# Strassen products for the second half's q, k and v; gates and the first projection as the attentions' filling

## The chip, the cores and the metric

The kernel runs on one core of one Trainium2 chip. A core has five engines, each with its own stream of instructions: TensorE (PE, matrix products and transpositions into PSUM), VectorE (DVE), ScalarE (ACT), GpSimd (POOL) and SyncE (SP, which here only issues transfers). They wait for each other through semaphores. The metric is the time on the device in microseconds, as the median of several runs; one further execution was profiled.

## The reference

One layer of an encoder on 2048 tokens with 1024 features, in float32. Cut to what matters:

```python
h = rms_norm(x, norm_mix)
z = h @ w_in                      # (2048, 1024) @ (1024, 4352)
q_a, k_a, v_a, q_b, k_b, v_b, g_a, g_b = split(z)   # 512,128,128,512,512,512,1024,1024
y_a = windowed_gqa(q_a, k_a, v_a, sink)       # 8 heads, 2 kv heads, |t-s| <= 128, ALiBi, sink logit
y_b = neighborhood_attn(q_b, k_b, v_b, rpb)   # 8 heads, 8 x 16 neighbours on a 32 x 64 grid, bias
gates = sigmoid(concat(g_a, g_b) + b_gate)
merged = gates[:, :1024] * (y_a @ w_proj_a) + gates[:, 1024:] * (y_b @ w_proj_b)
x = x + merged @ w_out
x = x + square(relu(rms_norm(x, norm_mlp) @ w_up)) @ w_down
return rms_norm(x, norm_final)
```

## The kernel before

**Arithmetic.** A float32 operand is held as a pair of `fp32r` numbers, high and low, and a product is three matmuls into one bank: high·high, high·low, low·high (`mm3`, lines 200 to 202, and `mm3s`, lines 284 to 286). So one "product" of a 128x128 weight tile and 512 tokens is always one matmul on each of three lines. Splitting a number in its pair costs a copy on ACT and a subtraction on DVE or POOL.

**Blocks.** The tokens lie in four blocks of 512 (`b` = 0 to 3). The first half is blocks 0 and 1, the second half 2 and 3.

**Dense stage (to 359.5 us).** For blocks 0 and 1, all columns of `w_in` come from "quads": a quad takes 512 columns (one takes 256) and both blocks, and forms the four quarter results with seven half-size products instead of eight (Strassen). `QUADS` lists them: k of A, q of A, q of B, k of B, v of B, four quads of gates. `in_seeded` runs a quad's products 1, 5, 6, 2, 7, 3, 4. Its right-hand operands are "pages" (`in_page[n]`, tiles `zh<n>`), one pair for each product `n`, made once from the normalised and transposed x; `in_left` makes the weight side (`zwhl`), `in_result` writes the results to DRAM. Beside the quads, `wo_parts` prepares `w_out` (in quads 2, 3, 7, 8), and in quads 5 and 6 blocks 2 and 3 of x are normalised and transposed into DRAM (`h1d`).

**Windowed attention A (359.5 to about 672 us) and neighbourhood attention B (to 1059.6 us)**, 32 units each (`attn_a`, `attn_b`). A unit computes scores on PE (bank `s`), bias and maximum on DVE, exponentials on ACT, normalisation on POOL, then for every 128 keys transposes on PE (bank `pt`), splits the result on ACT and DVE (`ph`, `pl`; in B `phb`, `plb`), and multiplies by v (bank `av`). `drive` starts units two ahead of the one that is finished. **Filling**: q, k, v and the gates of blocks 2 and 3 are computed during the attentions. `qk_tile`, `v_tile` and `gate_tile` are generators for 128 columns each; a generator loads its weights, splits them, then makes a piece of 24 matmuls (`feature_tile`, bank `mm`, with copy and store) for each of the two blocks, by full products. Their pages `hT` are loaded from `h1d`, scaled and split by `h_pages` at the start of A. `chain` strings the generators together and loads two ahead; `paced` puts one piece after the other into the program, each after the end of a stated unit (`done[at]`). The kernel's scheduler then sets the order of the instructions on each engine. In A there are 24 pieces, in B 44.

**Merge (1059.6 to 1393 us).** In two passes (`m` = 0: blocks 0 and 1, `m` = 1: blocks 2 and 3). `gated(f, n)` multiplies 128 columns of `w_proj_a` (n = 0) or `w_proj_b` (n = 1) by `y_a` or `y_b` (`load_y`), reads the gates from `zg`, applies the sigmoid, multiplies; the two are added to the pages `m0` to `m3`. Then `merged @ w_out` follows by Strassen (banks `b`, operands `pgl`), with the residual (`beside_out`). In pass 1, DVE also transposes the rows of the first pass for the MLP (`turned_out`, tiles `ht`, line 247) between the gated products.

**MLP.** The up stage runs to 2014 us, the down stage to the end; both are untouched.

## Time and profile before

| | us |
|---|---|
| median of 3 runs | 2634.39 (2632.62 to 2640.43) |
| profiled execution, its own time | 2636.0 |
| its span | 2634.2 |
| dense stage, after its start-up | 45 to 359.5 |
| attention A with the passage to it | 359.5 to about 672 |
| attention B | about 672 to 1059.6 |
| merge | 1059.6 to 1393 |
| up, down | 1393 to 2014, 2014 to 2634 |

In rows by windows, each engine's column is its busy time in the window and, in brackets, its instructions; then come the granted TensorE clock (1.00 is full), the mean busy share of the 16 DMA engines and the GB/s moved. With a tile's name given, only instructions on that tile are counted. In rows by groups stand line, engine, operation, output<-inputs, shapes and count, then busy us and mean ns of one, then the idle time just before them and what ended it. In rows of waits: engine, line, what was waited for, us in total, times, longest.

### The profile page before, as it was taken

The numbers are of one execution on the slowest core, as the hardware profiler recorded it, in microseconds if no ns is written. First come the engines' busy times: TensorE is split into PE (matmuls) and PEld (weight loads), VectorE is DVE, ScalarE is ACT, GpSimd is POOL, SyncE is SP. The second block draws the span as 40 slices with busy tenths as digits, with TensorE's granted clock in tenths as the row PEclk, the third lists the DMA queues.
The fourth block names the chain that finished last, engine by engine and source line by source line (L and its number), as shares of the span: only waits on it lengthen the run. The fifth ranks groups of instructions, "written<-read, shape, count | busy, mean of one in ns | idle before, by whom it ended". The sixth has DMA issues, their size and how long they took to land. (4 is left out here: it accounts for less than half of the span.)

```text
span 2634.2 us, 34479 instructions
## 1 busy us (share of the span) xinstructions
PE 2577.0 (98%) x12044; PEld 2138.2 (81%) x12044; DVE 1626.5 (62%) x2611; ACT 1290.9 (49%) x2319; POOL 374.1 (14%) x477
## 2 busy tenths in 40 slices
PE   8999999999999999999999999999999999999998
PEld 6878877787888888878887888888887888888887
DVE  7965566665444444465687677776656634554766
ACT  7445456666555555344246555644444322322444
POOL 0001233334555552000000000000000000000011
PEclk9999999999999999999999999999999999999999
DMA  5777785446777664777687655854427825444554
GB/s 184 246 245 205 237 277 148 116 125 177 212 222 198 174 186 138 268 240 235 202 296 239 237 204 199 283 200 148 149 103 289 314 98 183 147 147 169 184 192 168
DMA packets 349950, 525.94 MB, mean 200 GB/s; under 512 B 29624, under 2 KB 173112, under 8 KB 347600
## 3 DMA queue, kind: packets, MB, share of 16 engines
q1 hardware_dynamic: 333008, 483.88, 57.4%
q10 hardware_dynamic: 13248, 28.32, 2.9%
q0 software_dynamic: 3520, 11.54, 1.2%
q8 instruction: 95, 1.56, 0.2%
q14 instruction: 79, 0.65, 0.1%
HBM read 349.51 MB, written 174.13 MB: 199 GB/s over the span
## 5 line engine op out<-in xcount | busy, mean ns | idle before, releaser
L285 PE MATMUL b<-dwh,dah 128*128 128x512 f32 x896 | 349.0, 389 | 0.4 <-DVE dwh L281 0.4
L286 PE MATMUL b<-dwh,dah 128*128 128x512 f32 x896 | 348.1, 389 | 0.0
L284 PE MATMUL b<-dwh,dah 128*128 128x512 f32 x896 | 338.2, 389 | 1.7 <-ACT dwh L280 1.7
L280 ACT CAST dah<-da 128x1024 fp32r<-128x1024 f32 (+1 forms) x128 | 120.8, 945 | 368.3 <-PE b L286 250.3
L281 DVE TENSOR_TENSOR dah<-da,dah 128x1024 fp32r<-128x1024 f32 (+1 forms) x128 | 139.8, 1094 | 223.3 <-ACT dah L280 221.7
L284 PE MATMUL b<-ubh,uwhlb 128*128 128x512 f32 x592 | 232.1, 392 | 6.0 <-ACT uwhlb L280 4.4
L285 PE MATMUL b<-ubh,uwhlb 128*128 128x512 f32 x592 | 231.6, 391 | 0.6 <-DVE ubh L281 0.6
L286 PE MATMUL b<-ubh,uwhlb 128*128 128x512 f32 x592 | 229.7, 390 | 0.0
L200 PE MATMUL mm<-hT,whl 128*128 128x512 f32 x544 | 219.1, 403 | 3.5 <-ACT hT L754 3.5
L201 PE MATMUL mm<-hT,whl 128*128 128x512 f32 x544 | 215.2, 396 | 0.6 <-DVE hT L755 0.6
L202 PE MATMUL mm<-hT,whl 128*128 128x512 f32 x544 | 215.5, 396 | 0.0
L284 PEld LDWEIGHTS b<-dwh,dah 128*128 128x128 f32 x896 | 168.1, 188 | 36.9 <-ACT dwh L280 2.1
L285 PEld LDWEIGHTS b<-dwh,dah 128*128 128x128 f32 x896 | 168.2, 188 | 35.7 <-DVE dwh L281 0.8
L286 PEld LDWEIGHTS b<-dwh,dah 128*128 128x128 f32 x896 | 168.2, 188 | 34.8
L284 PE MATMUL zb<-zh,zwhl 128*128 128x512 f32 x476 | 187.1, 393 | 4.5 <-DVE zc L277 1.8
L285 PE MATMUL zb<-zh,zwhl 128*128 128x512 f32 x476 | 186.9, 393 | 0.0
L286 PE MATMUL zb<-zh,zwhl 128*128 128x512 f32 x476 | 185.6, 392 | 0.8 <-DVE zwhl L281 0.8
L277 DVE TENSOR_TENSOR uc<-b,uc 128x512 f32<-128x512 f32 x160 | 109.5, 690 | 122.7 <-PE b L286 116.5
L284 PEld LDWEIGHTS b<-ubh,uwhlb 128*128 128x128 f32 x592 | 111.8, 189 | 30.3 <-ACT uwhlb L280 4.8
L285 PEld LDWEIGHTS b<-ubh,uwhlb 128*128 128x128 f32 x592 | 111.9, 189 | 24.1 <-DVE ubh L281 1.0
L286 PEld LDWEIGHTS b<-ubh,uwhlb 128*128 128x128 f32 x592 | 111.4, 188 | 23.4
L200 PEld LDWEIGHTS mm<-hT,whl 128*128 128x128 f32 x544 | 102.9, 189 | 21.9 <-ACT hT L754 4.4
(268 smaller groups left out, 5838.6 us busy)
## 6 DMA issues: line engine op xcount, KB each, us to landing
at<-uc SPq DMA_DIRECT2D x224, 256.0 KB
da<-at SPq DMA_DIRECT2D x96, 512.0 KB
dw<-in_w_down_dram SPq DMA_DIRECT2D x160, 256.0 KB
uraw<-in_w_up_dram SPq DMA_DIRECT2D x32, 1024.0 KB
pgl<-wo_d SPq DMA_DIRECT2D x28, 1024.0 KB
raw<-in_w_in_dram SPq DMA_DIRECT2D x34, 512.0 KB
zraw<-in_w_in_dram SPq DMA_DIRECT2D x16, 1024.0 KB
z<-zg SPq DMA_DIRECT2D x64, 256.0 KB
```

Source lines behind the costliest of these rows:

```text
L200: PE.matmul(ps, lh, rh, start=first, stop=False)
L201: PE.matmul(ps, lh, rl, start=False, stop=False)
L202: PE.matmul(ps, ll, rh, start=False, stop=last)
L277: return eng.tensor_tensor(out=out, in0=a, in1=b, op=op).ins
L280: A.copy(hi, src)
L281: return eng.tensor_tensor(out=lo, in0=src, in1=hi.bitcast(F32), op=ALU.subtract).ins
L284: PE.matmul(ps, lh, rh, start=first, stop=False, skip_group_check=True)
L285: PE.matmul(ps, lh, rl, start=False, stop=False, skip_group_check=True)
L286: PE.matmul(ps, ll, rh, start=False, stop=last, skip_group_check=True)
```

## The change

The gates' and the first half's quads stay as they are, in another order. Five more quads follow for blocks 2 and 3: q of A, q of B, k of B, v of B, k and v of A. For their pages, x of blocks 2 and 3 is normalised and transposed two quads earlier (in quads 3 and 4); `h1_sums` reads `h1d` back in quads 5 to 7, forms the four sums and differences that Strassen needs and stores them (`h1s`); `h1_right` refills the pages in quad 8, the last one on the first half, product by product behind their last use; `h1_last` loads one more page that the gates of block 3 need. `w_out` is prepared in the later quads, the tables of B's bias in quad 11.

The filling is now 16 gate tiles for blocks 2 and 3, on the quads' pages, and then 8 `proj_tile`s: 128 columns of `w_proj_a` by `y_a`, all four blocks, two blocks (24 matmuls) a piece, multiplied by the gate and stored in DRAM as `zp`. 22 pieces lie in A, 26 in B. The merge multiplies by `w_proj_b` alone and adds `zp`.

A gate is no longer stored raw: ACT stores tanh of half its argument (`half_tanh`), and a sigmoid is half of that plus one. The "plus one" is an operand of the DVE multiplication, the half is a scale of 0.5 in the attentions' normalisation on POOL. Lastly, A loads K and V of both groups of heads at its start and takes its units in the order of groups 1, 0 throughout.

The diff, cut to its core:

```diff
+    def half_tanh(out, z, f):
+        A.activation(out, z, AF.Tanh, scale=0.5, bias=bg[:, f : f + 1])
...
-    QUADS = [(O_KA, P), (O_QA, 256), (O_QB, 256), (O_KB, 256), (O_VB, 256)]
-    QUADS += [(O_GA + n * BT, 256) for n in range(4)]
+    gate_quads = [(O_GA + n * BT, 256) for n in range(4)]
+    QUADS = [(O_KA, P), (O_QA, 256), (O_QB, 256), *gate_quads[:2], (O_KB, 256), (O_VB, 256), *gate_quads[2:]]
+    SECOND = len(QUADS)
+    QUADS += [(O_QA, 256), (O_QB, 256), (O_KB, 256), (O_VB, 256), (O_KA, P)]
...
+    G.tensor_scalar(bg[:, 0:16], bg[:, 0:16], 0.5, 1.0, ALU.mult, ALU.mult)
...
+    def h1_sums(k):
+        lo, hi = own(), own()
+        for t, p in ((lo, 0), (hi, 1)):
+            for j in range(2):
+                SY.dma_start(t[:, j * BT : (j + 1) * BT], h1d[j][p * BT + k * P : p * BT + (k + 1) * P, :])
...
+        for n, out, x, y in ((5, b11, b12, b11), (7, b12, b22, b12), (6, b22, b22, b11), (4, b21, b21, b22)):
+            yield
+            add(V, out, x, y, ALU.subtract)
+            G.dma_start(h1s[n][k * P : (k + 1) * P, :], out)
+    def h1_right(out):
+        for n in ORDER_3:
+            yield
+            b, p = {1: (0, 0), 2: (0, 1), 3: (1, 1)}.get(n, (None, None))
+            out[n] = h1_page(n, h1s[n]) if b is None else h1_page(n, h1d[b][p * BT : (p + 1) * BT], p)
...
-    h_pages(2)
-    def qk_tile(col, scale, tiled=False):
...
-    def v_tile(col):
...
-            G.tensor_scalar(s[:, h, lo:hi], s[:, h, lo:hi], ri[:, h : h + 1], 1.0, ALU.mult, ALU.mult)
+            G.tensor_scalar(s[:, h, lo:hi], s[:, h, lo:hi], ri[:, h : h + 1], 0.5, ALU.mult, ALU.mult)
...
+    def proj_tile(f):
+        raw = load_slice([(cols(w_pa[0], f * P), 4)])
+        yield
+        hl = T(wp, [P, 2, KC, P], F32R, "whl", 2)
+        split(raw[:, 0:4], hl[:, 0, 0:4], hl[:, 1, 0:4], V)
+        yield
+        for b in (0, 2):
+            z = T(wp, [P, 2, BT], F32, "z", 3)
+            for j in range(2):
+                SY.dma_start(z[:, j], zg[b + j][0][f * P : (f + 1) * P, :])
+            for j in range(2):
+                if ypages[b + j] is None:
+                    y_page(b + j)
+                hi, lo = ypages[b + j]
+                ps = psum("mm", 2)
+                for c in range(4):
+                    mm3(ps, hl[:, 0, c, :], hl[:, 1, c, :], hi[:, c], lo[:, c], c == 0, c == 3)
+                V.scalar_tensor_tensor(out=z[:, j], in0=z[:, j], scalar=1.0, in1=ps, op0=ALU.add, op1=ALU.mult)
+                put(zp[b + j][f], z[:, j])
+            yield
...
-    dense = [qk_tile(O_KA, 1.0), v_tile(O_VA)]
...
-    dense += [gate_tile(f, (2, 3)) for f in range(16)]
+    fill = [gate_tile(f, (2, 3)) for f in range(16)] + [proj_tile(f) for f in range(8)]
...
-    drive((attn_a(g, i) for g in (1, 0) for i in range(7)), live, False)
-    paced(fill, range(12), 24, 3)
...
-    drive((attn_a(g, i) for g in range(2) for i in range(7, 16)), live, True)
-    paced(fill, range(12, 24), 24, 3)
+    load_kv(1, 0)
+    load_kv(1, 1)
+    load_kv(0, 0)
+    load_kv(0, 1)
+    drive((attn_a(1, i) for i in range(14)), live, False)
+    paced(fill, range(11), 22, 3)
+    drive((attn_a(g, i) for g in (1, 0) for i in range(14 if g else 0, 16)), live, True)
+    paced(fill, range(11, 22), 22, 3)
...
-    paced(fill, range(20), 38, 4)
+    paced(fill, range(11), 21, 3)
...
-    paced(fill, range(20, 44), 38, 4)
+    paced(fill, range(11, 26), 21, 3)
...
-                V.tensor_tensor(out=g[:, j], in0=ps, in1=g[:, j], op=ALU.mult)
-            gates[f, n] = g
+                V.scalar_tensor_tensor(out=g[:, j], in0=g[:, j], scalar=1.0, in1=ps, op0=ALU.add, op1=ALU.mult)
+            add(V, ms[f // 2][:, f % 2], ga, g)
```

Three places in the order of the instructions, before and after. (Line numbers after are those of the changed kernel, two to some forty higher.)

PE at the end of the dense stage: the last quad's products (`zb<-zh4`) and the first products of the filling (`mm`). Before, with the pages `hT`:

```order
L285 MATMUL zb_75_2772<-zh4_62_594,zwhl_303_2741 128x512
L286 MATMUL zb_75_2772<-zh4_61_593,zwhl_303_2741 128x512
L284 MATMUL zb_75_2772<-zh4_61_593,zwhl_303_2741 128x512
L285 MATMUL zb_75_2772<-zh4_62_594,zwhl_303_2741 128x512
L286 MATMUL zb_75_2772<-zh4_61_593,zwhl_303_2741 128x512
L200 MATMUL mm_180_4068<-hT_320_3081,whl_334_3117 128x512
L201 MATMUL mm_180_4068<-hT_321_3082,whl_334_3117 128x512
L202 MATMUL mm_180_4068<-hT_320_3081,whl_334_3117 128x512
```

and after, PE at the same place:

```order
L286 MATMUL zb_111_4315<-zh4_311_2990,zwhl_462_4299 128x512
L287 MATMUL zb_111_4315<-zh4_312_2991,zwhl_462_4299 128x512
L288 MATMUL zb_111_4315<-zh4_311_2990,zwhl_462_4299 128x512
L397 MATMUL zb_114_4432<-ident_63,zc_472_4429 128x128 x4
L202 MATMUL mm_218_5462<-zh1_279_2740,whl_480_4525 128x512
L203 MATMUL mm_218_5462<-zh1_280_2741,whl_480_4525 128x512
L204 MATMUL mm_218_5462<-zh1_279_2740,whl_480_4525 128x512
```

The filling's first product now reads the quads' own pages (`zh1`); the four transpositions of v of A (line 397) stand ahead of it.

PE in B: `pt` are the transpositions of the probabilities, `s` the scores of a later unit, `av` the products with v, `mm` the filling. Before, in the middle of B:

```order
L202 MATMUL mm_675_10158<-hT_336_3122,whl_1313_10066 128x512
L200 MATMUL mm_675_10158<-hT_340_3136,whl_1313_10066 128x512
L201 MATMUL mm_675_10158<-hT_341_3137,whl_1313_10066 128x512
L202 MATMUL mm_675_10158<-hT_340_3136,whl_1313_10066 128x512
L200 MATMUL mm_675_10158<-hT_340_3136,whl_1313_10066 128x512
L1019 MATMUL pt_543_8623<-ident_63,sb1_1020_8390 96x128
L1019 MATMUL pt_543_8623<-ident_63,sb1_1021_8395 96x128 x2
L1019 MATMUL pt_543_8623<-ident_63,sb1_1022_8400 96x128
L991 MATMUL s_548_8680<-kb0_996_8273,qb_1048_8561 128x288 x2
L201 MATMUL mm_675_10158<-hT_341_3137,whl_1313_10066 128x512
L202 MATMUL mm_675_10158<-hT_340_3136,whl_1313_10066 128x512
```

and after, around the products `av_530` of one unit in B:

```order
L1068 MATMUL av_530_9250<-plb_1122_9256,vb1_1049_8659 128x128
L1057 MATMUL pt_532_9263<-ident_63,sb1_1053_8675 128x128
L1057 MATMUL pt_533_9276<-ident_63,sb1_1052_8670 128x128
L1057 MATMUL pt_533_9276<-ident_63,sb1_1053_8675 128x128 x2
L1057 MATMUL pt_533_9276<-ident_63,sb1_1054_8680 128x128
L1029 MATMUL s_538_9329<-kb0_1111_9205,qb_1114_9215 128x288 x2
L1068 MATMUL av_530_9250<-phb_1123_9268,vb1_1049_8659 128x256
L1029 MATMUL s_544_9403<-kb0_1111_9205,qb_1131_9309 128x384 x2
L1068 MATMUL av_530_9250<-plb_1124_9269,vb1_1049_8659 128x256
L1068 MATMUL av_530_9250<-phb_1123_9268,vb1_1049_8659 128x256
```

Between the transpositions of this unit and its value products no filling stands, only scores of later units; every unit of B had at least 20 filling matmuls before.

DVE in the second pass of the merge: `z<-b` reads a product's bank, `m0` is the merged page, `ht` the transposition for the MLP, `whl` a weight split. Before:

```order
L247 STREAM_TRANSPOSE ht_1490_12341<-xr_1394_11339 128x8x32
L252 TENSOR_TENSOR ht_1490_12341<-ht_1490_12341,gt_1357_10852 128x1024
L1500 TENSOR_TENSOR z_1484_12227<-b_47_12231,z_1484_12227 128x512
L1500 TENSOR_TENSOR z_1484_12227<-b_48_12245,z_1484_12227 128x512
L277 TENSOR_TENSOR m0_1476_12175<-z_1482_12185,z_1484_12227 128x1024
L177 TENSOR_TENSOR whl_1492_12354<-raw_1491_12351,whl_1492_12354 128x1024
L247 STREAM_TRANSPOSE ht_1495_12422<-xr_1375_11110 128x8x32
L247 STREAM_TRANSPOSE ht_1495_12422<-xr_1380_11183 128x8x32
L247 STREAM_TRANSPOSE ht_1495_12422<-xr_1385_11256 128x8x32
L247 STREAM_TRANSPOSE ht_1495_12422<-xr_1394_11339 128x8x32
L1500 TENSOR_TENSOR z_1488_12276<-b_49_12280,z_1488_12276 128x512
L252 TENSOR_TENSOR ht_1495_12422<-ht_1495_12422,gt_1357_10852 128x1024
```

and after, DVE at the same place:

```order
L1532 SCALAR_TENSOR_TENSOR z_1558_12651<-z_1558_12651,b_31_12657 128x512
L249 STREAM_TRANSPOSE ht_1565_12737<-xr_1480_11915 128x8x32
L249 STREAM_TRANSPOSE ht_1565_12737<-xr_1483_11952 128x8x32
L1532 SCALAR_TENSOR_TENSOR z_1558_12651<-z_1558_12651,b_32_12671 128x512
L249 STREAM_TRANSPOSE ht_1565_12737<-xr_1488_11995 128x8x32
L249 STREAM_TRANSPOSE ht_1565_12737<-xr_1491_12032 128x8x32
L179 TENSOR_TENSOR whl_1574_12805<-raw_1573_12802,whl_1574_12805 128x1024
L279 TENSOR_TENSOR m0_1548_12586<-z_1559_12652,z_1558_12651 128x1024
L254 TENSOR_TENSOR ht_1565_12737<-ht_1565_12737,gt_1455_11581 128x1024
```

A set of four transpositions now has two products beside it where it had four, and a sum `m0` after each two.

More of the change, by code (lines that the diff above doesn't have):

```diff
@@ L510, in in_seeded @@
             hl, (rh, rl) = next(lf), right[n]
-            for a in range(2):
+            for a in range(w // P):
                 if n == 1:
@@ new lines, in h1_page @@
+    def h1_page(n, src, p=None):
+        pages = in_page[n](), in_page[n]()
+        for half in range(2):
+            t = own().rearrange("p (k c) -> p k c", k=2)
+            SY.dma_start(t, src[half * 256 : (half + 1) * 256].rearrange("(k p) t -> p k t", p=P))
+            h, l = (halves(page)[half] for page in pages)
+            if p is None:
+                split(t, h, l, V)
+                continue
+            for k in range(2):
+                kk = 4 * p + 2 * half + k
+                scaled(h[:, k], t[:, k], kk)
+                scaled_less(l[:, k], t[:, k], kk, h[:, k].bitcast(F32))
+        return pages
@@ new lines, in h1_right, with h1_last, in_turn @@
+    def h1_right(out):
[3 more added lines that the diff above has]
+            out[n] = h1_page(n, h1s[n]) if b is None else h1_page(n, h1d[b][p * BT : (p + 1) * BT], p)
+    def h1_last(out):
+        for _ in range(4):
+            yield
+        out["b12"] = h1_page(6, h1d[1][0:BT], 0)
+    def in_turn(gens):
+        for g in gens:
+            yield from g
+    right2 = {}
+    for q in range(2, len(QUADS)):
+        prep, steps, b0 = iter(()), 1, 0
+        if q == 5:
+            prep = h1_sums(0)
+        elif q == 6:
+            prep = h1_sums(1)
+        elif q == 7:
+            prep, steps = in_turn((h1_sums(2), h1_sums(3))), 2
+        elif q == SECOND - 1:
+            prep = h1_right(right2)
+        elif q == len(QUADS) - 1:
+            prep = h1_last(right2)
+        elif q >= SECOND:
+            prep = wo_parts(q - SECOND, own)
+        if q == SECOND:
+            right, b0 = right2, 2
+        elif q > SECOND:
+            b0 = 2
+        next(prep, None)
+        if q == 11:
@@ L736, in encoder_layer @@
     wp = pools(s_w, "right", ("raw", "whl", "z"), "w")
-    s_h = ExitStack()
-    hpl = [pool(f"hT{n}", side="left", stack=s_h) for n in range(4)]
     s_a = ExitStack()
@@ L1097, in encoder_layer @@
     first_y = load_y(0)
-    for _ in range(3):
+    for _ in range(2):
         next_y = next(first_y)
-    paced(fill, range(20, 44), 38, 4)
+    paced(fill, range(11, 26), 21, 3)
+    flush(queue=SY)
     s_h.close()
```

218 lines of the change are left out of this document (80 added, 138 removed).

## The prediction

> **What bounds the kernel now.** I read the page first: the span, and each engine's share of it.
>
> ```profile
> span 2634.2 us, 34479 instructions
> PE 2577.0 (98%) x12044; PEld 2138.2 (81%) x12044; DVE 1626.5 (62%) x2611; ACT 1290.9 (49%) x2319; POOL 374.1 (14%) x477
> ```
>
> TensorE (PE) has 98% of the span. So the change is worth the matmuls that it takes away, less what it adds in stretches where PE isn't fed. For that I cut the span at its stages and asked for each engine's busy time in each piece; the piece 359.5 to 380 is the passage from the dense stage to the windowed attention (A), 1060 to 1393 is the merge.
>
> ```profile
> core 0: us, PE busy (x) PEld busy (x) DVE busy (x) ACT busy (x) POOL busy (x), PEclk, DMA share, GB/s
> 45.00:359.50 314.50, 310.20 (x1382) 254.96 (x1381) 220.76 (x283) 153.22 (x229) 39.26 (x60) 1.00 0.73 233
> 359.50:380.00 20.50, 16.43 (x65) 12.41 (x64) 7.81 (x15) 6.41 (x10) 3.80 (x7) 0.92 1.05 302
> 1060.00:1118.00 58.00, 58.00 (x257) 48.00 (x257) 28.47 (x34) 22.24 (x22) 0.00 (x0) 1.00 0.81 283
> 1118.00:1252.00 134.00, 130.93 (x569) 107.33 (x568) 86.02 (x120) 60.55 (x89) 4.40 (x8) 0.99 0.71 236
> 1252.00:1317.00 65.00, 65.00 (x289) 53.83 (x288) 41.54 (x59) 17.31 (x16) 0.00 (x0) 1.00 0.62 200
> 1317.00:1393.00 76.00, 74.85 (x329) 61.40 (x328) 61.16 (x81) 34.04 (x51) 3.28 (x6) 1.00 0.79 281
> 2014.00:2634.00 620.00, 610.29 (x2690) 504.49 (x2688) 357.41 (x496) 226.39 (x355) 14.59 (x17) 1.00 0.54 188
> ```
>
> Read two rows together. In 2014 to 2634, 2690 matmuls take 620 us, 0.230 us each; in 1060 to 1118, 257 take 58.0, 0.226. A 128x512 matmul therefore costs **0.227 us** of PE wherever PE is fed. That pitch, and not the mean duration of one record in the groups below (some 390 ns, since they overlap), is the unit of every sum here. The passage is the one place where PE visibly starves: 65 matmuls need 14.8 us and get 20.5, with a granted clock of 0.92.
>
> **Removed: matmuls.** Now the groups, per product line. Each product is written as three lines, so one line's count times three is the whole.
>
> ```profile
> L200 PE MATMUL mm<-hT,whl 128*128 128x512 f32 x544 | 219.1, 403 | 3.5 <-ACT hT L754 3.5
> L284 PE MATMUL zb<-zh,zwhl 128*128 128x512 f32 x476 | 187.1, 393 | 4.5 <-DVE zc L277 1.8 <-ACT zc L484 1.4 <-DVE ze L426 0.9
> L200 PE MATMUL b<-pgr,whl 128*128 128x512 f32 x128 | 50.0, 390 | 0.7 <-ACT z L899 0.7
> L200 PE MATMUL b<-pgs,whl 128*128 128x512 f32 x64 | 24.9, 389 | 0.0
> L200 PE MATMUL b<-pgl,whl 128*128 128x512 f32 x64 | 24.9, 389 | 0.0
> ```
>
> 544 is the attentions' filling, 476 the dense quads, 128+64+64 the gated products of the merge. The diff takes the q, k, v tiles (18 tiles, 2 blocks, 8 chunks: 288) out of the filling. It puts in five quads: four of 7 products, 4 chunks, 2 column tiles (56 each), and one of half the width (28), together 252. The projection with w_proj_a (128) only goes from the merge to the filling. The order of the changed kernel counts the same: 728 dense, 384 filling, 128 merge; 1240 a line against 1276. That is 36 x 3 = 108 matmuls, x 0.227 = **-24.5 us**, all on PE.
>
> **The passage.** The filling of before stands on pages that are loaded, scaled and split after the dense stage has ended:
>
> ```profile
> PE mm L200 <- ACT hT L754: 3.5, 2, 2.9
> PE pt L849 <- DVE pl L853: 2.9, 3, 1.8
> ```
>
> The first of these waits lies there, and with the clock it makes the 20.5 - 14.8 = 5.7 us. After, the pages are in SBUF when the quads end; the first gate tile needs only its weights. Three transfers of K and V are moved up on SyncE's queue, to A's start: the second waits for the dense stage's last stores of K and V, and behind it on that queue stand the other group's K and V and the fourth unit's q. Ahead of the first unit's value products A has 72 filling matmuls, 16.3 us, as cover; if that is too little, the passage keeps its loss. I leave 1 us: **-4.7** (0 to -5.7).
>
> **Dense stage, longer by 756 matmuls** (their PE time is in the count above). PE idles 314.5 - 310.2 = 4.3 us in 1382 matmuls there, so 2.4 in 756 more. VectorE (DVE) with 220.76 of 314.5 is no bound; the added page sums and splits sit in 38 us quads. Each page of the second half is filled into the buffer that the last quad on the first half reads, one quad ahead of its use; the wait for a late page is not in the trace. It is bounded by 0 and by what the passage lost to the same pages, 5.7. I take 1.9, near 0, since a quad of cover lies between: together **+4.3** (2.4 to 8.1). The 16 stores of the page sums are issued by GpSimd, which has 39.26 of 314.5 us there.
>
> **Attentions: less filling.** The filling falls from 544 to 384 a line, so from 48 x 34 = 1632 matmuls to 1152, over the same 64 units. Its matmuls vanish at their pitch (counted). What is not counted is a unit that is left with next to nothing beside it, a bare unit below. By the order, units with 8 filling matmuls or fewer ahead of their value products: 7 of 32 in A before and 10 after; none in the neighbourhood attention (B) before and **11** after. What such a unit costs, A shows. First all engines, then the filling alone, in the same windows: 431.6 and the last four of the second list are single bare units; 404.9 to 653.4 holds 28 units and 702.8 to 1005.5 holds 26 of B.
>
> ```profile
> 404.90:653.40 248.50, 240.08 (x1233) 196.62 (x1233) 159.63 (x431) 159.30 (x416) 95.18 (x128) 0.99 0.50 135
> 702.80:1005.50 302.70, 302.70 (x1767) 266.74 (x1766) 143.11 (x372) 171.60 (x415) 155.65 (x170) 1.00 0.68 191
> 504.10:511.60 7.50, 6.96 (x35) 4.79 (x34) 5.33 (x18) 7.36 (x24) 2.08 (x4) 1.00 0.50 133
> 574.60:582.50 7.90, 7.55 (x41) 5.47 (x40) 6.81 (x20) 7.83 (x25) 2.81 (x5) 1.00 0.69 184
> ```
> ```profile
> 404.90:653.40 248.50, 129.63 (x512) 93.22 (x511) 0.00 (x0) 0.00 (x0) 0.99 0.50 135
> 702.80:1005.50 302.70, 193.12 (x763) 139.06 (x764) 0.00 (x0) 0.00 (x0) 1.00 0.68 191
> 431.60:440.70 9.10, 0.20 (x1) 0.23 (x2) 0.00 (x0) 0.00 (x0) 0.81 0.68 189
> 504.10:511.60 7.50, 1.46 (x6) 1.24 (x7) 0.00 (x0) 0.00 (x0) 1.00 0.50 133
> 539.60:547.00 7.40, 1.59 (x7) 1.36 (x8) 0.00 (x0) 0.00 (x0) 1.00 0.57 161
> 574.60:582.50 7.90, 1.22 (x5) 1.05 (x6) 0.00 (x0) 0.00 (x0) 1.00 0.69 184
> 610.50:617.90 7.40, 1.47 (x6) 1.24 (x7) 0.00 (x0) 0.00 (x0) 1.00 0.54 152
> ```
>
> Take the filling off at 0.227. The four units from 504.1 on keep 6.14, 5.81, 6.77 and 6.04 us, mean 6.19; the one at 431.6 keeps 8.87. The 28 units together keep 248.5 - 512 x 0.227 = 132.3; less those five (33.6), the other 23 have 98.7, or 4.29 each. A bare unit of A costs 1.9 more than a filled one, and ScalarE (ACT) is why: busy 7.36 of 7.5, 7.83 of 7.9. Three more of them: **+5.7** (0 to 13.7, each at the price of 431.6).
>
> B keeps (302.7 - 763 x 0.227) / 26 = 4.98 us a unit, with ACT at 171.6 / 26 = 6.6 each. Alone, a unit of B is then ACT's and lies between 4.98 (ACT had worked ahead) and 8.87 (the row at 431.6). I take 6.3, by the nearest rows (6.19 in A, where ACT also ends the unit): 11 x 1.3 = **+14.3** (0 to 42.8).
>
> **Merge.** With w_proj_a gone, 384 of its matmuls leave, and with them 87 of the 333 us. Left beside them is the vector work of the second half, one set of four transpositions a feature tile, of which before:
>
> ```profile
> L1500 DVE TENSOR_TENSOR z<-b,z 128x512 f32<-128x512 f32 x30 | 20.0, 682 | 12.3 <-PE b L202 12.3
> L277 DVE TENSOR_TENSOR m<-z,z 128x1024 f32<-128x1024 f32 x8 | 9.8, 1225 | 0.2
> L177 DVE TENSOR_TENSOR whl<-raw,whl 128x1024 fp32r<-128x1024 f32 x6 | 7.3, 1219 | 5.8 <-ACT whl L176 5.8
> L252 DVE TENSOR_TENSOR ht<-ht,gt 128x1024 f32<-128x1024 f32 x6 | 7.3, 1214 | 0.1
> L247 DVE STREAM_TRANSPOSE ht<-xr 128x256 f32<-128x256 f32 x20 | 7.2, 415 | 7.7 <-DMA h2d<-ht 7.7
> ```
>
> After, a feature tile has 24 matmuls, 5.45 us, where it had 48. DVE has two products at 0.682 (taking the fused multiply at the plain one's price), the sum 1.225, half a weight split 0.61, four transpositions 1.66 and the gain 1.21: 6.07. DVE becomes the longer by 0.6 a tile, 8 tiles: 5. The waits for the one transposition buffer (7.7) are DVE's idle time and now count too, but sets stand before the first and after the last product, and the output products follow without DVE work. I take **+2** (-3, the 134.0 - 130.93 that PE idles in 1118 to 1252, to +10). The merge's sigmoids become tanh in the filling, one for one in the place of copies, and the other edits (0.5 for 1.0 as a scale on GpSimd, the gate bias scaled once, K and V of A loaded at once) put no instruction on PE: 0, covered by GpSimd's 14%.
>
> **Sum:** -24.5 - 4.7 + 4.3 + 5.7 + 14.3 + 2 = -2.9 us. The profiled execution took 2636.0 (span 2634.2 and 1.8 around it), the median of the runs is 2634.4; I take the sum off the median: **2631.5**. A difference of 0.3%, 7.9 us, is about what a measurement of this kernel can tell from none: faster is below 2626.5, slower above 2642.3.
>
> **Rivals.** *Faster: bare units cost nothing.* ACT has 6.6 us a unit of B against 4.98 + 24 x 0.227 = 10.4 in a filled one, so it may work ahead over the two or three units in flight and absorb a bare one. For it: 302.70 of 302.7 busy in B. Against: in A, where units are begun two ahead as well, ACT ended such units. Then -24.5 - 4.7 + 4.3 + 2 = -22.9: 2611.5.
>
> *Slower: the clock drops at bare units.* At 431.6 PE waits 1.8 us for `pl` (above), and this window has the clock at 0.81:
>
> ```profile
> 431.60:440.70 9.10, 7.07 (x33) 5.55 (x32) 7.18 (x18) 7.63 (x23) 3.72 (x5) 0.81 0.68 189
> ```
>
> If each bare unit of B leaves PE waiting so, it costs 8.87 - 4.98 = 3.9 and not 1.3: 42.8 for 14.3, so 2660; with five of eleven, 2644.5. It decides from a wait of some 1.8 us. Against: the four others of A kept the clock at 1.00. The Trainium skill ("TensorE: Matmul & The Clock Gate", "A second HAM failure mode: psum-queue depth-cycling") says that frequent short idles of PE between groups of matmuls make the clock swing between full and half; its section "HAM oscillation — how this bites in real kernels" puts the danger at idles over 3.4 us. By the first the bare units throttle, by the second they don't; here one of five did, after 1.8 us, so the trace stands between them.
>
> *Slower: the merge becomes the DMA's.* Its four rows carry 16.4 + 31.6 + 13.0 + 21.4 = 82.4 MB. The loads of y_a and of w_proj_a go (4.2 MB each); zp comes in for a gate that left, and some last stores of zp run in: 76 MB in 333 - 87 = 246 us, 309 GB/s. At the 283 of 1060 to 1118 it takes 269: +23, 2654.5. It decides from about 300 GB/s over the merge. Against:
>
> ```profile
> 1060.00:1080.00 20.00, 20.00 (x89) 16.54 (x89) 10.96 (x14) 6.80 (x8) 0.00 (x0) 1.00 1.04 391
> 1320.00:1340.00 20.00, 19.15 (x84) 15.23 (x82) 17.05 (x17) 11.94 (x16) 0.00 (x0) 1.00 1.03 394
> ```
>
> The queues reach 390 where they have the work. That the matmuls don't go isn't open: the order counts them.
>
> **How the numbers follow.** Forecast 0.49, bare units free 0.25, clock 0.13, merge by DMA 0.13. The forecast's own range, 2620 to 2643, comes from B's price between 0.4 and 2.3 a unit. Of it a fifth lies below 2626.5 and little above 2642.3; of the clock's and the DMA's cases five sixths lie above. Faster 0.25 + 0.10 = 0.35, slower 0.22 + 0.02 = 0.24, same 0.41. A range of 2609 to 2657 leaves out the far part of the free case (its dense and passage terms at their good ends) and of the clock case, 0.1 each.
>
> **What would show it.** Right: a dense stage of some 314.5 + 756 x 0.227 + 4 = 490 us and no wait of 3 us behind it; A and B shorter by their 480 matmuls (109 us) less some 20; in B bare windows of 6 to 7 us with ACT nearly full and a clock of 1.00; a merge near 248 us. Wrong: bare units of 5 us (the first rival), PEclk of 0.9 or less in B (the second), `pgl` or `z` loads as releasers of PE in the merge (the third), or page loads that hold up the quads on blocks 2 and 3.

## The result and the profile after

The changed kernel takes **2676.07 us** (2674.47 to 2679.78, 4 runs) against 2636.04 for the kernel before on the same chip: ratio 1.0153, 95% interval 1.0133 to 1.0173, so 1.5% slower. Its profiled execution has a span of 2672.7 us against 2634.2, 38.5 more.

The page of the changed kernel, the span and the engines:

```profile
span 2672.7 us, 34547 instructions
PE 2578.7 (96%) x11936; PEld 2127.9 (80%) x11936; DVE 1703.9 (64%) x2700; ACT 1308.6 (49%) x2349; POOL 335.3 (13%) x460
```

PE has 108 matmuls fewer (12044 to 11936) and is busy as long as before: it waits more, and works at a lower clock in part of B. Windows by stage show where. First the changed kernel (dense, A, B, merge, MLP), then the same five stages of the kernel before:

```profile
core 0: us, PE busy (x) PEld busy (x) DVE busy (x) ACT busy (x) POOL busy (x), PEclk, DMA share, GB/s
0.00:541.80 541.80, 521.01 (x2327) 425.01 (x2328) 369.24 (x466) 295.41 (x442) 47.58 (x77) 1.00 0.73 230
541.80:829.90 288.10, 273.77 (x1387) 223.19 (x1385) 165.13 (x476) 181.52 (x480) 103.49 (x148) 0.98 0.45 126
829.90:1182.10 352.20, 314.17 (x1771) 266.76 (x1770) 206.54 (x499) 192.93 (x482) 160.89 (x202) 0.94 0.77 217
1182.10:1434.40 252.30, 247.56 (x1081) 203.20 (x1080) 182.76 (x249) 87.72 (x131) 7.69 (x14) 0.99 0.87 308
1434.40:2672.70 1238.30, 1222.17 (x5377) 1009.77 (x5375) 780.21 (x1011) 551.06 (x816) 15.70 (x19) 1.00 0.56 193
```
```profile
0.00:359.50 359.50, 344.09 (x1532) 281.77 (x1533) 250.44 (x326) 190.25 (x299) 45.25 (x76) 1.00 0.72 230
359.50:672.00 312.50, 298.21 (x1503) 241.71 (x1502) 194.88 (x528) 196.91 (x516) 123.22 (x170) 0.99 0.56 153
672.00:1059.60 387.60, 382.05 (x2197) 333.37 (x2195) 183.13 (x454) 217.66 (x511) 182.23 (x199) 1.00 0.68 191
1059.60:1393.00 333.40, 329.06 (x1438) 270.84 (x1439) 217.19 (x292) 134.20 (x178) 7.69 (x14) 0.99 0.73 247
1393.00:2634.20 1241.20, 1223.57 (x5379) 1010.53 (x5377) 780.82 (x1011) 551.90 (x816) 15.68 (x19) 1.00 0.55 192
```

The filling alone in A and in B, of the changed kernel (its pages `zh`; the eight operations of DVE and ACT are the splits of y) and of the one before (`hT`):

```profile
541.80:829.90 288.10, 147.22 (x576) 105.48 (x576) 0.00 (x0) 0.00 (x0) 0.98 0.45 126
829.90:1182.10 352.20, 139.44 (x552) 101.43 (x552) 10.43 (x8) 8.29 (x8) 0.94 0.77 217
```
```profile
359.50:672.00 312.50, 165.25 (x648) 119.79 (x649) 5.99 (x8) 5.34 (x8) 0.99 0.56 153
672.00:1059.60 387.60, 248.07 (x986) 179.15 (x984) 0.00 (x0) 0.00 (x0) 1.00 0.68 191
```

Take the moved and removed matmuls off at 0.227 us, and each stage shows what it lost beside them. Dense: 541.8 - 359.5 = 182.3, less 756 x 0.227 = 171.6, leaves +10.7. A without its filling: 157.3 against 165.4, -8.1. **B without its filling: 352.2 - 125.3 = 226.9 against 387.6 - 223.8 = 163.8, +63.1.** Merge: -81.1, of which -81.7 are matmuls (384 less, 24 of filling ran into it): +0.6. MLP -2.9. A part of this is only the place of the cut. The 40 transpositions of v (6.0 us of PE, rows further down) went from A's filling to the dense stage, so that this stage lost some 4.7 and not 10.7 of its own. And before, 22 of B's 256 score matmuls (5.5 us) ran in A's window; so A lost some 3 of its own, where the rows show -8.1, and of B's 63.1 some 5 are this shift.

In B the clock is 0.94 where it was 1.00: of the 352.2 us at most 6%, 21 us, are lost to the clock itself (an estimate from that row; a part of it fell on waits). PE's waits in B, after and then before:

```profile
PE av L1068 <- DVE yb L1077: 8.8, 6, 2.4
PE s L1029 <- DMA qb<-qs_b: 7.8, 1, 7.8
PE s L1029 <- DVE stb L1034: 5.6, 9, 2.1
PE pt L1057 <- DVE plb L1063: 5.2, 6, 1.8
```
```profile
PE s L991 <- DMA kb<-ks_b: 1.6, 1, 1.6
PE s L991 <- DVE stb L996: 1.3, 2, 1.0
```

Cut at its two worst places, B of the changed kernel is:

```profile
829.90:860.00 30.10, 16.80 (x59) 13.51 (x58) 9.64 (x30) 8.38 (x24) 12.58 (x14) 0.60 0.79 216
860.00:960.00 100.00, 95.85 (x573) 81.73 (x572) 57.37 (x152) 63.28 (x159) 64.65 (x80) 1.00 0.80 208
960.00:1020.00 60.00, 48.16 (x263) 38.95 (x262) 39.15 (x85) 36.81 (x88) 26.50 (x31) 0.94 0.86 253
1020.00:1182.10 162.10, 153.36 (x881) 132.57 (x880) 100.38 (x232) 84.46 (x214) 57.17 (x79) 0.96 0.71 209
```

These rows hold 5, 170, 73 and 309 filling matmuls and 1, 10, 5 and 16 units (16 value products each). With the filling off at 0.227 and the units off at the 5.12 us that they took before (163.8 / 32), an estimate of the loss is 23 us at the entry, 18 where the filling changes from gates to projection, and 20 in the other 262 us together.

Three things stand out in the trace after. **The entry into B.** SyncE's and PE's rows of the timeline at the end of A: the first masks and q of B are issued after A's last value product (829.85), and B's first scores come 7.75 us later.

```profile
829.85 0.39 PE L869 MATMUL av<-pl,va 128*128 128x512 f32 x1
830.26 0.35 SPq L979 DMA_DIRECT2D masks<-in_mask_b_dram  x1
830.66 1.38 SPq L1016 DMA_DIRECT2D qb<-qs_b  x2
837.99 4.41 PE L1029 MATMUL s<-kb,qb 128*128 128x288 f32 x14 [7.75 <-DMA qb<-qs_b]
```

SyncE's waits name that value product as what the masks were issued after (L979 <- PE L869, 0.6 us). Before, B's scores ran beside A's last units, as at 655.03 (the first stood at 643.18), while A's last value product came at 673.91:

```profile
655.03 0.52 PE L991 MATMUL s<-kb,qb 128*128 128x384 f32 x2
673.91 0.39 PE L855 MATMUL av<-pl,va 128*128 128x512 f32 x1
```

**The change from gates to projection.** ScalarE's waits in B, and the longest on its timeline: a cast of a y page stands in ScalarE's stream before its load has landed, and the attention behind it.

```profile
ACT zh L282 <- DMA raw<-y_a: 14.2, 6, 6.1
962.74 1.05 ACT L282 CAST zh<-raw 128x1024 fp32r<-128x1024 f32 x1 [6.10 <-DMA raw<-y_a]
```

**Bare units.** Three units with 0, 2 and 0 filling matmuls, by windows; the clock falls in all of them. The first lies at the change to the projection.

```profile
966.90:977.80 10.90, 8.51 (x40) 7.21 (x40) 7.61 (x18) 7.49 (x17) 6.44 (x7) 0.69 0.78 259
1099.30:1106.50 7.20, 5.86 (x32) 5.72 (x33) 3.91 (x11) 5.01 (x14) 6.05 (x8) 0.76 0.59 175
1145.90:1152.30 6.40, 5.01 (x23) 5.01 (x24) 4.69 (x9) 4.19 (x9) 2.11 (x4) 0.53 0.44 115
```

### The profile page after: what moved, and what is told of

The parts are those of the page before. It is cut to its first block, busy times and chain, and to the rows that moved or that the text cites. A ratio compares the mean times of both kernels' runs of the same rounds, so it can differ in the third digit from the quotient of the medians.

```text
span 2672.7 us, 34547 instructions
## 1 busy us (share of the span) xinstructions
PE 2578.7 (96%) x11936; PEld 2127.9 (80%) x11936; DVE 1703.9 (64%) x2700; ACT 1308.6 (49%) x2349; POOL 335.3 (13%) x460
## 5 line engine op out<-in xcount | busy, mean ns | idle before, releaser
L286 PE MATMUL zb<-zh,zwhl 128*128 128x512 f32 x728 | 285.8, 393 | 7.9 <-ACT zb L532 2.4
L288 PE MATMUL zb<-zh,zwhl 128*128 128x512 f32 x728 | 283.8, 391 | 1.2 <-DVE zwhl L283 1.2
L287 PE MATMUL zb<-zh,zwhl 128*128 128x512 f32 x728 | 284.8, 391 | 0.0
L286 PEld LDWEIGHTS zb<-zh,zwhl 128*128 128x128 f32 x728 | 136.7, 188 | 41.6 <-ACT zb L532 3.9
L288 PEld LDWEIGHTS zb<-zh,zwhl 128*128 128x128 f32 x728 | 136.8, 188 | 30.8 <-DVE zwhl L283 2.7
L287 PEld LDWEIGHTS zb<-zh,zwhl 128*128 128x128 f32 x728 | 136.8, 188 | 27.4
L202 PE MATMUL mm<-zh,whl 128*128 128x512 f32 x384 | 156.0, 406 | 0.6 <-ACT zh L282 0.6
L204 PE MATMUL mm<-zh,whl 128*128 128x512 f32 x384 | 151.6, 395 | 0.0
L203 PE MATMUL mm<-zh,whl 128*128 128x512 f32 x384 | 150.7, 392 | 0.3 <-DVE zh L283 0.3
L286 PEld LDWEIGHTS b<-ubh,uwhlb 128*128 128x128 f32 x592 | 111.6, 189 | 29.2 <-ACT uwhlb L282 3.8
```

Of the source, the lines that this page charges most:

```text
L202: PE.matmul(ps, lh, rh, start=first, stop=False)
L203: PE.matmul(ps, lh, rl, start=False, stop=False)
L204: PE.matmul(ps, ll, rh, start=False, stop=last)
L286: PE.matmul(ps, lh, rh, start=first, stop=False, skip_group_check=True)
L287: PE.matmul(ps, lh, rl, start=False, stop=False, skip_group_check=True)
L288: PE.matmul(ps, ll, rh, start=False, stop=last, skip_group_check=True)
```

## The experiments

Ratios are to the kernel before on the same chip, as recorded with their intervals (not quotients of the medians); the changed kernel has 1.0153.

| run | edit | us | ratio, 95% |
|---|---|---|---|
| e1 | no y pages | 2664.4 | 1.0112 (1.0097 to 1.0128) |
| e2 | even filling | 2667.4 | 1.0112 (1.0083 to 1.0141) |
| e3 | old order of groups | 2665.4 | 1.0116 (1.0101 to 1.0131) |
| e4 | e3, late K and V | 2666.3 | 1.0119 (1.0103 to 1.0134) |
| e5 | gate stores on SyncE | 2675.6 | 1.0158 (1.0142 to 1.0174) |
| e6 | y pages in place | 2682.9 | 1.0174 (1.0156 to 1.0191) |
| e7 | e2 + e3 + e5 + e6 | 2654.7 | 1.0074 (1.0059 to 1.0089) |
| e8 | before, half gate products | 2575.1 | 0.9776 (0.9760 to 0.9792) |
| e9 | e7, casts held | 2642.6 | 1.0020 (1.0011 to 1.0030) |
| e10 | e9, V in the filling, casts later | 2642.4 | 1.0019 (1.0009 to 1.0028) |
| e11 | e10, stores on ScalarE | 2642.0 | 1.0011 (0.9997 to 1.0025) |
| e12 | e9, gates loaded ahead, casts spread | 2643.4 | 1.0036 (1.0024 to 1.0048) |
| e13 | e11, gates loaded ahead | 2645.5 | 1.0041 (1.0024 to 1.0057) |
| e14 | changeover repairs alone | 2676.4 | 1.0160 (1.0145 to 1.0175) |
| e15 | e2 + e3 + e5, no y pages | 2629.4 | 0.9981 (0.9967 to 0.9994) |

The theory at the start: B is lost at these three places. The rivals: VectorE, which took over the projection's multiplications; SyncE's queue; plain lack of filling.

**e1, no y pages.**

```diff
-                if ypages[b + j] is None:
-                    y_page(b + j)
-                hi, lo = ypages[b + j]
+                hi, lo = right2[(1, 2, "b12", 3)[b + j]]
```

> The changed kernel without the loading and splitting of the y pages for the projection in the filling (the products read the pages of x that are there; that part of the computation is left out, all matmuls stay). Theory: ScalarE stands in its stream behind casts that wait for these loads (waits of 14.2 us in B, 6.1 us the longest), and the attention behind it; then the time falls by 15 to 20 us against the changed kernel, to about 2658. Rival: the loss in B comes from units without filling; then only the casts themselves go, and the time falls by less than 5.

Measured 0.4% less than the changed kernel, 11 us: the theory's side, two thirds of its size. The edit takes loads, casts and subtractions away together; it doesn't tell them apart.

**e2, even filling.**

```diff
-            feature_tile(ps, hl, hp[b])
+            feature_tile(ps, hl, hp[b], 0, 4)
+            yield
+            feature_tile(ps, hl, hp[b], 4, 8)
...
                 put(zp[b + j][f], z[:, j])
-            yield
+                yield
...
-    paced(fill, range(11), 21, 3)
+    paced(fill, range(20), 42, 3)
```

> The changed kernel with its filling cut in pieces of 12 matmuls instead of 24, handed out at the same rate, so that hardly a unit of A or B is left without filling (11 such units in B before, 1 now, the first of B). Theory: a unit without filling costs B 1.2 to 2 us and its neighbours wait too; then the time falls by 20 to 30 us against the changed kernel, to about 2650. Rival: B is lost to VectorE, which now does the projection's multiplications and splits, or to waits for loads; then the time stays within 5 us of the changed kernel.

Some 10 us less (11 by the ratios, 8 by the medians; its runs lie between 2657 and 2672), half of what was expected and twice what the rival had. Taking the gaps out of the filling leaves units of 12 matmuls, and these aren't quite free either (e8).

**e3, the old order of groups, and e4, late K and V.** The edit of e3 (one of the four loads of K and V also moves behind two others); e4 loads the second half's K and V after the first seven units of each group:

```diff
-    drive((attn_a(1, i) for i in range(14)), live, False)
+    drive((attn_a(g, i) for g in (1, 0) for i in range(7)), live, False)
...
-    drive((attn_a(g, i) for g in (1, 0) for i in range(14 if g else 0, 16)), live, True)
+    drive((attn_a(g, i) for g in range(2) for i in range(7, 16)), live, True)
```

> The changed kernel with A's units in the old order of groups (1, 0, then 0, 1), the K and V loads still all at A's start. Theory: the tables and the q of B lie in SBUF over the tiles of group 0, which the changed kernel uses to the end of A, so that B's first units can't start beside A's last ones; then the passage from A to B (830 to 858 us) loses 14 to 18 us less, and the time is about 2660. Rival: the passage is bound by the empty filling there or by SyncE's queue; then within 4 us of the changed kernel.

> As the kernel with the old order of groups, and K and V of the second half loaded after the first seven units of each group, as in the kernel before. Theory: the burst of K and V loads at A's start holds a store issued by ScalarE, and with it the first units (ScalarE idle 8.8 us, PE 7.7 us and then half clock); then 6 to 10 us less than the kernel with the old order alone, about 2652. Rival: the wait there is for what the last quads store; then the same time as with the old order alone.

e3 gained 10 us, and its trace shows the mechanism: B's first scores at 815.37, beside A's last units, instead of 837.99.

```profile
815.37 0.73 PE L1029 MATMUL s<-kb,qb 128*128 128x288 f32 x3
```

e4 came out as e3, as its rival had it, but tells nothing: its K and V loads stand at the same place of SyncE's stream (the last of them at 562.04, in e3 at 559.58), since nothing in the program holds them back.

**e5, gate stores on SyncE.**

```diff
-            A.dma_start(zg[b][f // 8][(f % 8) * P : (f % 8 + 1) * P, :], z)
+            put(zg[b][f // 8][(f % 8) * P : (f % 8 + 1) * P, :], z)
```

> The changed kernel with the filling's gate stores issued by SyncE, with the next unit's store, instead of by ScalarE as soon as the gate is there. Theory: ScalarE's issue of the second gate store waits 8.8 us for a transfer at A's start, and the attention's exponentials queue behind it; then the passage into A loses 6 to 8 us less, and the time is 2668 or a little below the changed kernel's. Rival: what is late there is K, q or the probabilities' tables themselves; then within 3 us of the changed kernel.

No gain, the rival's side. PE's waits at A's start, in the changed kernel and in e5, say why: the wait for ScalarE is gone and one for q stands in its place.

```profile
PE av L868 <- ACT ph L866: 7.7, 1, 7.7
```
```profile
PE s L844 <- DMA qa<-qs_a: 9.7, 1, 9.7
```

**e6, y pages in place, and e7, all together.** The y pages' loads no longer go through the weights' buffers but into the page itself, right behind the last gate product:

```diff
+            if f == 15:
+                for y in range(2 * b - 4, 2 * b - 2):
+                    y_load(y)
...
-            split(raw, halves(hi)[g], halves(lo)[g], V)
+            split(halves(lo)[g].bitcast(F32), halves(hi)[g], halves(lo)[g], V)
```

> The changed kernel with the y pages loaded right behind the last gate products, straight into the page that will hold the low parts, and split there; nothing is left out. Theory: with the loads one to two units ahead, ScalarE's casts no longer wait for them (14.2 us in B); then most of the 12 us of the run without y pages is gained, and the time is about 2665. Rival: the cost of the y pages is the casts and subtractions themselves (8 of about 1 us on ScalarE, 8 of 1.2 us on VectorE); then within 4 us of the changed kernel.

> The changed kernel with all repairs together: even filling, old order of groups in A, gate stores on SyncE, y pages loaded ahead and in place. The single runs gave 9, 11 and up to 12 us. Theory: the losses lie in different places of A and B and add up; then about 2640, still not below the kernel before. Rival: they share the same slack (a unit that is late anyway hides another's wait); then 2650 or more.

e6 gained nothing: ScalarE still waits 15.1 us for these loads (14.2 in the changed kernel). In e7 ScalarE's timeline shows the same: the cast still stands ahead of its load's landing, now by 13.87 us. The scheduler's order put it there. e7's time (2654.7) is on the rival's side, but not by the rival's reason: e2 and e3 gained 0.4% each, e5 and e6 nothing, and all four together 0.8%, so the gains add up and share no slack that can be seen.

```profile
938.02 1.04 ACT L282 CAST zh<-zh 128x1024 fp32r<-128x1024 f32 x1 [13.87 <-DMA zh<-y_a]
```

**e8, the kernel before with thinner filling.** This takes every part of the change away but one.

```diff
-            feature_tile(ps, hl, hp[b])
+            feature_tile(ps, hl, hp[b], 4)
```

> The kernel before with half of each gate product of the filling left out (4 of 8 chunks; the gates of blocks 2 and 3 are wrong then): 384 matmuls fewer, 87 us of TensorE, all in B, whose filling falls from 943 to 571 matmuls, in pieces of 12, spread evenly. Theory: B needs about 20 filling matmuls a unit to keep TensorE fed, and one with 12 loses about 1 us; then the time falls by 60 to 70 us only, to about 2570. Rival: thin but even filling costs nothing, and the changed kernel loses B by its gaps and its loads alone; then by 83 to 88, to about 2549.

The time falls by 58.7 us where 87.2 us of matmuls went, close to the theory's 60 to 70 and far from the rival's 83 to 88: **28 us are lost when the filling is thinned and nothing else is changed**, with the old order of groups, no y pages and no bare units. Windows of it: all of B, a stretch that waited, the 60 us round it and the 100 us behind; below, the waits in that stretch, PE's for ScalarE and ScalarE's own, which the profile puts down to a transfer of K.

```profile
672.00:999.40 327.40, 308.67 (x1814) 266.92 (x1813) 180.49 (x452) 216.07 (x509) 181.78 (x199) 0.97 0.82 224
817.60:833.20 15.60, 11.73 (x64) 9.90 (x63) 6.14 (x17) 6.91 (x18) 7.53 (x9) 0.86 0.97 223
792.00:852.00 60.00, 53.66 (x314) 45.62 (x314) 32.12 (x83) 37.65 (x93) 34.38 (x40) 0.94 0.82 220
852.00:952.00 100.00, 97.62 (x604) 84.58 (x604) 62.53 (x164) 74.71 (x182) 68.16 (x77) 1.00 0.88 237
PE av L1030 <- ACT phb L1024: 3.9, 1, 3.9
ACT phb L1024 <- DMA kb<-ks_b: 5.6, 1, 5.6
```

With the same transfers in a shorter B, the DMA share rises from 0.68 to 0.82. The cast that waits 5.6 us doesn't read K; just ahead of it in ScalarE's stream stands the issue of a gate store (at 829.52), so it was probably that issue which was held until the transfer landed. ScalarE's hold reaches PE, and the clock falls (0.86).

The loss isn't even. The 60 us hold 86 filling matmuls and 6 units, the 100 us behind them 163 and 11.6 (186 value products): beside its filling a unit took 6.7 us in the first and 5.4 in the second, against 5.12 before. So some 10 of the 28 us lie round one hold, and thin filling where nothing is late costs some 0.3 us a unit (the theory had 1), 10 for all 32 (estimates from these rows). e15, below, agrees.

**e9, casts held.** The casts are queued behind ScalarE's own copies of units 11, 11, 12, 13:

```diff
+            with tc.issue_after(ends[(11, 11, 12, 13)[b]]):
+                split(halves(lo)[g].bitcast(F32), halves(hi)[g], halves(lo)[g], V)
```

> The kernel with all repairs, and ScalarE's casts of the four y pages queued behind its last copy of units 11, 11, 12 and 13 of B, one to two units after their loads are issued. Theory: in that run ScalarE stood 13.9 us in front of such a cast whose load had been issued 6 us after the cast's turn came, and the four units there lost some 29 us to 4; with the casts behind the units the stretch loses less than 10, and the time falls from 2655 to about 2633, level with the kernel before. Rival: the projection's products wait for the casts all the same and PE runs bare there; then 2645 to 2652.

0.5% less than e7 and 0.2% above the kernel before (clear of noise), half of the expected gain and between theory and rival: a part of the wait went on to VectorE, which now stands before a multiplication whose gate hasn't landed (waits of 936 to 976 us):

```profile
DVE z L958 <- DMA z<-zg: 8.4, 1, 8.4
```

**e10 and e11, V in the filling.** The quad of V for blocks 2 and 3 is taken out and made by full products; the casts are held two units longer than in e9, and a part of `w_out` is prepared in quad 2:

```diff
-    QUADS += [(O_QA, 256), (O_QB, 256), (O_KB, 256), (O_VB, 256), (O_KA, P)]
+    QUADS += [(O_QA, 256), (O_QB, 256), (O_KB, 256), (O_KA, P)]
...
+    fill = [v_tile(O_VB + t * P) for t in range(4)] + [gate_tile(f, (2, 3)) for f in range(16)] +
```

> The kernel with all repairs and held casts, with V of the neighbourhood attention for blocks 2 and 3 taken out of the quads and put back into the filling, by full products (24 matmuls more, 5.4 us), so that A and B have about 21 filling matmuls a unit instead of 17. Theory: the half-gate run lost 28 us to a filling of 12 a unit, so that filling is worth more than what Strassen saves on it; then 10 to 15 us less than the run with held casts, below the kernel before. Rival: what is left in A and B is latency that filling doesn't hide, and the 5.4 us come on top; then 2638 or more.

> As the run with V in the filling, with the gate stores issued by ScalarE as in the changed kernel. Theory (the store's issue holds ScalarE for a transfer): 3 to 8 us slower than with the stores on SyncE. Rival (alone, moving the stores gained nothing, since on SyncE they hold the loads behind them): the same within 3 us.

Both on the rivals' side: what the filling gives, its matmuls cost.

**e12, e13 and e14, the gates loaded ahead.** In e12 and e14 the casts are also held behind units 11, 12, 13 and 14.

```diff
+        zs = {0: gates_of(f, 0)}
         yield
...
-            z = T(wp, [P, 2, BT], F32, "z", 3)
-            for j in range(2):
-                SY.dma_start(z[:, j], zg[b + j][0][f * P : (f + 1) * P, :])
+            z = zs[b]
```

> The kernel with all repairs and held casts, in which the projection's gates are also loaded a piece or more ahead of their multiplication, and the four y pages' casts are spread over units 11 to 14. Theory: in the run with held casts VectorE then stood 8.4 us in front of a multiplication whose gate had not landed (unit of 12.7 us lost), the same fault one engine further on; with that load ahead, two units there lose some 20 us to 6 or so, and the time falls from 2643 to 2628 to 2633, a little below the kernel before. Rival: the loads are late because SyncE's queue and the DMA are full there, so that another wait takes its place; then 2640 or more.

> The run with V in the filling (stores by ScalarE), with the gates of the projection loaded ahead. Theory: as for the run before, 10 us off 2642, about 2632; V in the filling is then worth what it costs. Rival: 2640 or more.

> The changed kernel as it is (uneven filling, its own order of groups), with only the change from gates to projection repaired: y pages in place, casts held, gates loaded ahead. Theory: the four units around that change (966 to 1013 us of its trace) lose 18 us there and would lose 5 to 6; 12 us or more less than the changed kernel, about 2662. Rival: units without filling beside them keep PE waiting there anyway; then 2670 or more.

All three on the rivals' side. Windows of e12 at the changeover: the DMA share is 1.0 for 60 us. In 915 to 985 us VectorE still waits 4.9 us for a gate (`z <- zg`), though it is loaded ahead.

```profile
920.00:940.00 20.00, 19.92 (x125) 17.41 (x124) 12.56 (x33) 11.95 (x31) 7.65 (x11) 1.00 1.02 254
940.00:960.00 20.00, 16.73 (x89) 14.89 (x86) 14.27 (x29) 14.99 (x33) 14.63 (x14) 0.83 1.07 335
960.00:980.00 20.00, 14.69 (x83) 12.39 (x84) 12.66 (x29) 8.86 (x22) 6.11 (x7) 0.98 0.97 220
```

**e15, the repairs without y pages.** The edit is e1's, on e2, e3 and e5.

> Even filling, the old order of groups and gate stores on SyncE, without loading and splitting the y pages (the products read the pages of x that are there; that part of the computation is left out, all matmuls stay); the projection's gates are loaded as in the changed kernel. Theory: what three attempts on the order of casts and loads left at the change from gates to projection (units of 6 to 8 us excess, with the DMA engines' share at 1.0 from 920 to 980 us) is the burst of 4 MB of y loads itself; without it the time is 10 to 14 us under the run with gates ahead, about 2631. Rival: the wait for the projection's gates stays; then 2638 or more.

14 us less than e12, the theory's size. The same windows of e15:

```profile
940.00:960.00 20.00, 19.80 (x122) 17.38 (x121) 13.07 (x34) 14.20 (x37) 15.04 (x20) 1.00 0.95 245
960.00:980.00 20.00, 18.91 (x120) 16.49 (x119) 14.63 (x36) 11.47 (x29) 8.91 (x11) 1.00 0.86 239
844.00:1024.00 180.00, 177.29 (x1093) 155.14 (x1092) 117.05 (x305) 118.04 (x304) 109.79 (x138) 1.00 0.85 230
```

PE is fed there, and VectorE waits 1.5 us for a gate where e12 has 4.9. So the y pages' step costs 14 us even after its order was repaired (which was worth 12, e7 to e9). That it is the 4 MB of loads, in a stretch with a DMA share of 1.0, fits these waits but isn't shown alone: the casts and subtractions went with them. The last row holds 319 filling matmuls and 20 units: 16 a unit, and 5.4 us a unit beside them at a clock of 1.00. Thin filling that is even, with nothing late beside it, costs little.

## Why the prediction was wrong

**Matmuls, -24.5: right.** 12044 to 11936, all 108.

**The merge, +2: within its bounds** (+0.6). VectorE's longer tiles didn't reach PE, which waited once for `z` there, 0.6 us. The merge moved 308 GB/s over its 252.3 us, so the third rival (DMA from 300 GB/s on) is refuted.

**The dense stage, +4.3: too low** (+10.7, outside its bounds), by an omission: the transpositions of v moved with it, and their 6.0 us with them. What is left, 4.7, is near the forecast. Groups before (dense stage, filling) and after:

```profile
L395 PE MATMUL zb<-ident,zc 128*128 128x128 f32 x40 | 6.0, 272 | 0.0
L395 PE MATMUL mm<-ident,z 128*128 128x128 f32 x40 | 6.0, 272 | 0.0
L397 PE MATMUL zb<-ident,zc 128*128 128x128 f32 x80 | 12.1, 273 | 1.5 <-DVE zc L279 0.8 <-ACT zc L457 0.7
```

**The passage, -4.7: wrong; A's bare units, +5.7: can't be told.** PE lost the passage again, 7.7 us before `ph`, behind the 72 matmuls that were to cover it. The sum had the K and V loads delay a later unit; ScalarE's waits at A's start, which the profile puts down to them, stand before the first unit's `ph`:

```profile
ACT sta L849 <- DMA ka<-ks_a: 10.8, 2, 8.8
```

In ScalarE's stream a gate store stands just ahead of the instruction that waits here; without that store (e5) the wait is PE's, for q. A as a whole lost some 3 of its own, passage and three more bare units together, where the two terms had +1.0; that this is near is luck, since the passage came out the wrong way.

**B, +14.3: the step that failed.** It measured +63.1, some 58 without the shift between the windows, above the bound of 42.8. The term counted bare units and priced each. That price was low, but not the main fault: of the three windows above, the two away from the change took 7.2 us (6.7 without two filling matmuls) and 6.4, against the 6.3 forecast, and all of B outside its two worst places lost 20 us. The other 40 lie in places for which the sum has no term.

First, it looked for waits inside a unit and not between stages. The new order of groups isn't mentioned in the sum, so it stood at nothing. The tables and q of B lie over group 0's tiles in SBUF (`biasa0`, `va0`, `ka0`: both sets are laid out from the same side), and the last user of those now sets when B may begin: some 23 us at the entry, of which e3 gives back 10.

Second, the projection in the filling was priced by its matmuls. Its four pages bring 4 MB and eight casts into B's middle: some 18 us there; 11 come back alone (e1), 14 beside the other repairs (e15).

Third, the row of B before (302.7 busy of 302.7) was read as the length of B's own work, whatever lies beside it. It was the length under a cover that hid every hold and late load. With half of the gate products gone e8 lost 28 us without a bare unit: some 10 round one hold of ScalarE, some 10 as 0.3 us a unit.

Together: taking these away (even filling, e3's order, no y pages; with e5's stores, which gain nothing alone) brings the changed kernel from 1.0153 to 0.9981, 45 us, though without the y pages it computes something else. What is then left of the 24.5 us is 5; the other 19 or so weren't measured by themselves (the dense stage's 4.7 and thin filling are parts of them).

**The second rival (the clock): its clock came true where units are quite bare, its price didn't.** The clock is 0.69, 0.76 and 0.53 in the three windows above, behind waits of 1.4, 1.8 and 2.4 us (`av <- yb`, PE's first row of waits in B). But the two bare units away from the change took 7.2 and 6.4 us, where this rival had 8.9. The Trainium skill ("TensorE: Matmul & The Clock Gate", "A second HAM failure mode: psum-queue depth-cycling") describes a clock that swings between half and full when PE idles shortly and often between groups of matmuls. Here one wait of 1.8 or 2.4 us was enough, though not every one was (1.8 us at 1012.5 left the clock at 1.00). The Trainium skill ("TensorE: Matmul & The Clock Gate", "HAM oscillation — how this bites in real kernels") has the rule that no idle should be longer than some 3.4 us. These waits are shorter, so that rule was too lax here. In all three windows the wait began before the clock fell, so the clock made the loss longer and didn't start it. **The first rival** (bare units are free) is refuted in B; A doesn't decide it.

Open: what held ScalarE at the gate stores, whether the loads or the casts of the y pages cost the 14 us, and where the rest of e8's 28 us lies. No full version beat the kernel before: e9 and e10 are 0.2% slower, e11 can't be told from it (1.0011), with 108 (e9) or 84 matmuls fewer.

## What to carry to other kernels

Filling in a bound engine's stream is also the cover of everything that is late beside it. Before it is thinned, look for the waits of the *other* engines in the covered stretch, and for the DMA share: they cost nothing there now, and come to the surface when the cover goes. Price an operation that is moved into such a stretch by its loads and casts as well as its matmuls, and a change of order by what SBUF places the next stage's first tiles over.

## What the hardware showed that was not expected

An engine that helps with the filling carries the filling's late loads into the attention behind it in its stream: one cast on ScalarE stood 13.87 us before a load (e7). Holding it back gained 12 us, but a part of the wait turned up on VectorE (8.4 us in e9, 4.9 in e12, where the DMA share was 1.0). And one wait of PE of 1.8 or 2.4 us was enough for a clock of 0.76 or 0.53 in the unit around it.
